# A two-layer conditioned decoder trunk on one core: another order for the opening, swaps of the first rotary tiles by ScalarE, weight loads and score banks arranged anew

## The chip, the cores and the metric

The kernel runs on one core of one Trainium2 chip. The metric is device time in microseconds for one execution of the whole program; lower is better. The engines are named as in the profile: PE (TensorE, matrix products and transposes), DVE (VectorE), ACT (ScalarE), POOL (GpSimd) and SP (SyncE, which here only issues DMAs).

## The reference

Two layers work on `x` (512 rows of 1024, float32), conditioned by a vector `c`:

```python
c_act = silu(c)
for l in range(2):
    ada = c_act @ w_ada[l] + b_ada[l]                  # six pieces of 1024: shift, scale, gate, twice
    h = rmsnorm(x, norm_mix_g[l]) * (1 + sc_m) + sh_m
    a_in, b_in, q, k, v, gate_pre = split(h @ w_in[l])
    y_a, y_b = two convolution branches (a_in, b_in)
    q, k = apply_rope(q, cos, sin), apply_rope(k, cos, sin)   # 8 heads, 2 x 64 each
    o = diff_attention(q, k, v, lam)                   # softmax 0 minus lam * softmax 1, causal
    y_c = rmsnorm(o) @ w_c_out[l]
    x = x + g_m * ((g_a * y_a + g_b * y_b + g_c * y_c) @ w_out[l])
    h = rmsnorm(x, norm_mlp_g[l]) * (1 + sc_f) + sh_f
    x = x + g_f * (relu(h @ w_ff1[l]) ** 2 @ w_ff2[l])
return rmsnorm(x, final_g)
```

The rotary step turns each 64-wide half of a head by an angle `position * inv_freq`: `[t1*cos - t2*sin, t2*cos + t1*sin]`.

## The kernel before

Activations lie transposed: 128 features on the partitions by 512 rows of `x` in the free dimension, so `x` and `h` are 8 tiles of 128x512 each. Every float32 operand is split into a high part (an ACT cast) and a low part (a DVE subtraction), and a product is three passes, high by high, low by high, high by low, of 128x512 matmuls (24 for one output tile of 128 features; `proj`, L145).

**Weights.** `raw_issue` lets SP load 128x8x256 of a weight matrix (1 MB) into one of two `raw` buffers. `w_split` turns one half of a raw buffer (`hh` 0 or 1) into `wh` (ACT, L394) and `wl` (DVE, L402); after the second half it calls `raw_issue`, so the next 1 MB load is issued as soon as the program comes past that point, and waits for the last reader of the buffer.

**Order.** Each engine works through its instructions in the order in which the program emits them. Python generators ("tasks") are spawned with a delay in steps; a step passes with each 4096 columns of matmul (eight 128x512 matmuls). `yield n` in a task lets n steps pass before its next part is emitted. So a task's yields set what stands ahead of what on each queue.

**The opening** is written out by hand, as the string `START` of units. `x` turns a tile of `x` by PE and copies it by ACT (`v`: by DVE), `y` sums squares, `i` loads and turns the parameter rows `prm` (L207), `a` are the steps of the rotary angles (the last one emits the `Sin` activations, sin_t and cos_t), `e` and `d` are the parts of the adaLN products that DVE makes (rows of `w_ada` times a column of `cact`; table `ON_DVE` says how many of 8 k-tiles, for four quarters `qt` and the two vectors scale and shift), `r`, `s` the rest of these products on PE (`rows_of`, L1193), `c`, `t`, `q` copy, turn and store the quarter's result, `m` modulates two tiles of `h`, `h` and `l` split a quarter of the first four weight tiles, and `p` is one of 16 partial products: quarter `qt` of tile `i`. The four tiles are q and k of heads 0 and 1. SP's stream in the opening is 256 KB pieces: positions, 8 of `x`, then per quarter 8 of `w_ada` and 2 of `w_in`. After `START` come 1 MB loads.

**Rotary** (`rope`, L706): ACT copies the product from PSUM, SP issues four DMAs that swap the 32-row groups into `sw`, DVE multiplies by cos_t and, 2 steps later, `sw` by sin_t, adds, and after that the result is split and pieces of it are moved by DMA into the layout of the scores (L738, L739).

**Attention.** `mixer` makes for each pair of heads four product tiles (q, k, q, k), then the values. `attend` makes for each head and row block i of four the scores of both softmaxes (L789, L790), each in a PSUM bank of its own of the two `s` banks:

```python
            sps = [ps_s(), ps_s()]
```

`softmax` masks them on DVE (L754), takes exp on ACT (L761) and combines both on DVE (L770). Then PE turns the combined blocks (L806), and the products with the values follow.

Of the kernel before, what the change touches and what calls it, by code (L numbers as in the profile page):

```python
# [17 lines left out]
P = 128  # L18
# [14 lines left out]
WDELAY = 1  # L33
LAM = 2

ON_DVE = ((2, 3), (1, 5), (8, 3), (3, 7))
START = (
# [4 lines left out]
)  # L42
QSTEP, COMB, AWAIT, PWAIT, PERIOD = 2, 2, 3, 4, 9
CPACE, ADA0, ADA1, APACE = 0.71, 2.36, 2.19, 1.62
ADA_BR = 0
FIRST = 2
RWAIT = 2


RDELAY = (0, 1, 1)  # L50
# [21 lines left out]
def kernel(  # L72
# [158 lines left out]
    def lambdas():  # L231
        lq, lk = slot("at", F32, [1, L, 2, 64]), slot("at", F32, [1, L, 2, 64])
        for j, (a, b) in enumerate(((lam_q1, lam_k1), (lam_q2, lam_k2))):
            G.dma_start(lq[:, :, j, :], a[None, :, :])
            G.dma_start(lk[:, :, j, :], b[None, :, :])
        yield 15
        V.tensor_tensor(lq, lq, lk, op=ALU.mult)
        ls, le, ll = stile(4), stile(4), stile(2)
        V.tensor_reduce(out=ls[0:1, :], in_=lq.rearrange("p l j d -> p (l j) d"), op=ALU.add, axis=AX.X)
        ones = ftile(F32, [1, P])  # L240
        V.memset(ones, 1.0)
        yield 1
        A.activation(le[0:1, :], ls[0:1, :], AF.Exp)
        yield 1
        for l in range(L):
            V.scalar_tensor_tensor(
                out=ll[0:1, l : l + 1], in0=le[0:1, 2 * l + 1 : 2 * l + 2], scalar=-lam_init[l],
                in1=le[0:1, 2 * l : 2 * l + 1], op0=ALU.add, op1=ALU.subtract)
        yield 2
        pt = ps_t()  # L250
        T.matmul(pt[:, 0:2], ones, ll[0:1, :], start=True, stop=True)
        yield 1
        V.tensor_copy(nlam, pt[:, 0:2])
        written.add("lam")
# [103 lines left out]
            chunks += [(len(specs) + g, hh) for hh in range(2) for g in range(len(grp))]  # L358
            specs += grp
    raws, wready = [], []  # L360
    wnext, spare = [0], set()

    def raw_issue():
        if len(raws) < len(specs):
# [6 lines left out]
    def w_split(extra=None):  # L371


        if wnext[0] >= len(chunks):
            return
        n, hh = chunks[wnext[0]]
        wnext[0] += 1
        raw, kk = raws[n], specs[n][2]
        if kk < 0:

            shape, rs = [P, 4, 256], raw[:, 4 * hh : 4 * hh + 4, :]
            n_k = 4
        else:
            shape, rs = [P, 8, P], raw[:, :kk, hh * P : (hh + 1) * P]
            n_k = kk
        if extra:
            half = [P, n_k // 2] + shape[2:]
            his = [slot(extra, F32R, half) for _ in range(2)]
            parts = [(hf, rs[:, i * half[1] : (i + 1) * half[1], :]) for i, hf in enumerate(his)]
        else:  # L390
            hi = wpool.tile(shape, F32R, tag="wh", name=nm("wh"))
            parts = [(hi[:, :n_k, :], rs)]
        for h_, r_ in parts:
            A.copy(h_, r_)  # L394
        yield 1
        if extra:
            los = [slot(extra, F32R, half) for _ in range(2)]
        else:
            lo = wpool.tile(shape, F32R, tag="wl", name=nm("wl"))
            los = [lo[:, :n_k, :]]  # L400
        for l_, (h_, r_) in zip(los, parts):
            V.tensor_tensor(l_, r_, h_.bitcast(F32), op=ALU.subtract)  # L402
        wready.append(([h_[:, k, :] for h_, _ in parts for k in range(n_k // len(parts))],
                       [l_[:, k, :] for l_ in los for k in range(n_k // len(parts))], extra))
        if hh == 1:
            raw_issue()

    def getw():
# [62 lines left out]


    xT = [xpool.tile([P, S], F32, name=f"xT{k}") for k in range(KD)]

    def modulate(l, f, rb, hh, ks, t0=0, t1=S):

        sv = (SH_M if f == 0 else SH_F) * 8
        assert all(q + k in ada_known[l] for k in ks for q in (sv, sv + 8))
        n = t1 - t0
        u = {}  # L480
        for k in list(ks) + [None]:
            if k is not None:
                u[k] = ftile()
                V.scalar_tensor_tensor(
                    out=u[k][:, :n], in0=xT[k][:, t0:t1], scalar=gsc[l][:, f * 8 + k : f * 8 + k + 1],
                    in1=rb[:, :n], op0=ALU.mult, op1=ALU.mult)
                A.activation(hh[k][0][:, t0:t1], u[k][:, :n], AF.Identity,
                             bias=ada[l][:, sv + k : sv + k + 1])
            if len(u) > (1 if k is not None else 0):
                j = min(u)  # L490
                V.scalar_tensor_tensor(
                    out=hh[j][1][:, t0:t1], in0=u.pop(j)[:, :n], scalar=ada[l][:, sv + j : sv + j + 1],
                    in1=hh[j][0][:, t0:t1].bitcast(F32), op0=ALU.add, op1=ALU.subtract)

    def new_h():
        return [(slot("h", F32R), slot("h", F32R)) for _ in range(KD)]
# [207 lines left out]
    cos_t = const.tile([P, S], F32, name="cos_t")  # L704
    sin_t = const.tile([P, S], F32, name="sin_t")

    def rope(pp, res, j):

        t, sw = ftile(), ftile()
        A.copy(t, pp)
        for q in range(4):
            nc.sync.dma_start(sw[32 * q : 32 * q + 32, :], t[32 * (q ^ 1) : 32 * (q ^ 1) + 32, :])  # L714
        yield 1
        u = ftile()
        V.tensor_tensor(u, t, cos_t, op=ALU.mult)
        yield 2
        V.tensor_tensor(sw, sw, sin_t, op=ALU.mult)  # L719
        V.tensor_tensor(u, u, sw, op=ALU.add)  # L720
        yield 1
# [58 lines left out]
    def attend(l, hd, q, k, v, res):  # L780
# [2 lines left out]
        l0 = stile(4)  # L783
        for i in range(NTB):
            n = (i + 1) * P
            sps = [ps_s(), ps_s()]
            blk = slice(i * P, (i + 1) * P)
            for cc in range(2):
                T.matmul(sps[cc][:, :n], q[cc][:, blk], k[cc][:, :n], start=True, stop=False)  # L789
                T.matmul(sps[cc][:, :n], q[2 + cc][:, blk], k[cc][:, :n], start=False, stop=True)  # L790
            spawn(softmax(l, i, sps, l0, a))
            yield QSTEP
# [54 lines left out]
    def mixer(l, h, qk, nfirst):  # L847
# [15 lines left out]
                yield PERIOD  # L863

        spawn(heads())
        for hp in range(NH // 2):
            if hp:
                qk, nfirst = [], 0
# [162 lines left out]
        def branch(pp, br, e, tg):  # L1031
# [6 lines left out]
            else:  # L1038
# [2 lines left out]
                yield 1  # L1041
                yield from split(m[e], merged)

        for br, act in enumerate((oo, yb, ya)):
            hold[0] = False
            if br == ADA_BR and l == 0:
                spawn(ada_task([(0, v) for v in (G_M, SH_F, SC_F, G_F)] +
                               [(1, v) for v in (SC_M, SH_M, G_M, SH_F, SC_F, G_F)], lambda: pace["ada"]))
            for j in range(4):
                tg = []  # L1050
                for e in (2 * j, 2 * j + 1):
                    product(h, gate, br, e, tg)
                    product(act, branch, br, e, tg)
# [45 lines left out]
    rc = const.tile([P, 2], F32, name="rc")  # L1099
    A.dma_start(rc, rope_c)  # L1100
    posi = slot("at", I32)
    nc.sync.dma_start(posi, positions.to_broadcast([P, S]))
    prm_task = params(0)
    next(prm_task)
    x2 = x.rearrange("b s d -> (b s) d")
# [19 lines left out]
    for qt in range(4):  # L1125
        quarters.append((fetch(SC_M, qt), fetch(SH_M, qt)))
        for raw, (src, c0, _) in zip(raws, specs):
            nc.sync.dma_start(raw[:, 2 * qt : 2 * qt + 2, :],
                              src[256 * qt : 256 * qt + 256, c0 : c0 + 256].rearrange("(k p) e -> p k e", p=P))

    pt = ps_t()
    T.transpose(pt[:, :8], crow, ident[:8, :8])
# [38 lines left out]
    def part(qt, v):  # L1171
        return parts[qt % 2][:, v * 256 : v * 256 + 256]

    def partial(qt, vs):

        for k in range(8):
            for v in vs:
                k0 = 8 - ON_DVE[qt][v]
                if k < k0:
                    continue  # L1180
                r = quarters[qt][v][k // 2][:, k % 2, :]
                if k == k0:
                    V.tensor_scalar(out=part(qt, v), in0=r, scalar1=cact[:, k : k + 1],
                                    scalar2=None, op0=ALU.mult)
                else:
                    V.scalar_tensor_tensor(out=part(qt, v), in0=r, scalar=cact[:, k : k + 1],
                                           in1=part(qt, v), op0=ALU.mult, op1=ALU.add)

    def rows_of(qt, v, pt):

# [45 lines left out]
        V.tensor_scalar(out=ms, in0=ms, scalar1=1.0 / D, scalar2=None, op0=ALU.mult)  # L1236
        box["y0"] = rstd(ms, 4)

    w1, qk, q_rows, q_cols, w_tasks = [], [], {}, {}, []
    first = {}  # L1240
    box = {}
    ang_task, lam_task = angles(), lambdas()
# [37 lines left out]
    def first_product(qt, i):  # L1280
# [6 lines left out]
        proj(first[i], w1[i], h, 0, S, 2 * qt, 2 * qt + 2)  # L1287
        if qt == 3:
            release(w1[i])
            spawn(rope(first[i], qk, i))  # L1290
            run_due()

    def rows_scale(qt):
# [3 lines left out]
    def rows_copy(qt):  # L1297
        row = ftile()
        A.copy(row, q_rows[qt])
        q_rows[qt] = row  # L1300

    units = dict(
        x=lambda k: x_turned(k, A),
        v=lambda k: x_turned(k, V),
# [2 lines left out]
        z=lambda _: next(lam_task),  # L1307
        a=lambda _: next(ang_task, None),
        b=lambda _: box.update(rb=bcast(box["y0"], 4)),
        e=lambda qt: partial(qt, (0,)),  # L1310
        d=lambda qt: partial(qt, (1,)),
        f=lambda qt: partial(qt, (0, 1)),
        r=rows_scale,
        s=lambda qt: rows_of(qt, 1, q_rows[qt]),
        c=rows_copy,
        t=lambda qt: q_cols.update({qt: turn(q_rows[qt])}),
        q=lambda qt: quarter_done(qt, q_cols[qt]),
        m=lambda qt: modulate(0, 0, box["rb"], h, (2 * qt, 2 * qt + 1)),
        h=high, l=low,
        p=lambda n: first_product(n // 4, n % 4),  # L1320
    )
# [7 lines left out]
    for l in range(L):  # L1329
# [6 lines left out]
        f = mlp(l, h, f, NF)  # L1336
        if l + 1 < L:
            qk = []
            h = closing(l, G_F, f, l + 1, 0, lambda pp, i: rope(pp, qk, i))
    ending(f)  # L1340
    while tasks:
        step()
# [35 lines left out]
```

## Time and profile before

| | |
|---|---|
| median of 3 runs | 1908.89 us (1908.52 to 1911.45) |
| profiled execution | 1904.28 us, of which 1902.5 us are the span of the trace |
| PE busy | 1874.3 us, 99% of the span |
| DVE, ACT, POOL busy | 1256.0, 785.8, 63.4 us |
| DMA | 241.20 MB, 127 GB/s mean |

The span is the trace from the first to the last instruction; 1.8 us of the profiled execution's time lie around it. A row of the timeline gives the start, the busy time, the engine with the line and operation, output<-input, and in brackets how long the engine sat idle before it and whose event ended that. PE rows of several matmuls overlap in their records, so that a row of six 128x512 matmuls of 0.39 us each lasts 1.53 us.

### The profile page before, as it was taken

The numbers are of one execution on the slowest core, as the hardware profiler recorded it, in microseconds if no ns is written. First come the engines' busy times: TensorE is split into PE (matmuls) and PEld (weight loads), VectorE is DVE, ScalarE is ACT, GpSimd is POOL, SyncE is SP. The second block draws the span as 40 slices with busy tenths as digits, with TensorE's granted clock in tenths as the row PEclk, the third lists the DMA queues.
The fourth block names the chain that finished last, engine by engine and source line by source line (L and its number), as shares of the span: only waits on it lengthen the run. The fifth ranks groups of instructions, "written<-read, shape, count | busy, mean of one in ns | idle before, by whom it ended". The sixth has DMA issues, their size and how long they took to land.

```text
span 1902.5 us, 24972 instructions
## 1 busy us (share of the span) xinstructions
PE 1874.3 (99%) x9565; PEld 1599.9 (84%) x9565; DVE 1256.0 (66%) x2139; ACT 785.8 (41%) x1420; POOL 63.4 (3%) x109
## 2 busy tenths in 40 slices
PE   8999999999999999999999999999999999999998
PEld 6788888888889888888898888888888898888888
DVE  7788789996676556565677777898654563333336
ACT  4466652223333524333445666322243353424253
POOL 1011010000000000000000000000000000000000
PEclk9999999999999999999999999999999999999999
DMA  8644323444554455555535442232233422223221
GB/s 272 181 130 126 101 67 98 151 138 145 166 178 135 139 178 195 177 185 182 171 97 142 123 122 73 89 104 96 67 100 100 133 89 89 89 93 106 89 89 67
DMA packets 211527, 241.20 MB, mean 127 GB/s; under 512 B 10408, under 2 KB 178480, under 8 KB 211408
## 3 DMA queue, kind: packets, MB, share of 16 engines
q1 hardware_dynamic: 210480, 239.38, 40.6%
q8 instruction: 75, 1.23, 0.3%
q0 software_dynamic: 768, 0.23, 0.1%
q14 instruction: 44, 0.36, 0.1%
q10 hardware_dynamic: 160, 0.01, 0.0%
HBM read 216.50 MB, written 2.10 MB: 115 GB/s over the span
## 4 chain that ended last, share of the span: by engine, by line
PE 93%; DMA 3%; DVE 2%; issue 1%; SPq 1%; ACT 1%; POOL 0%; POOLq 0%; DVEq 0%; ACTq 0%
PE mm L145 83%; PE s L145 3%; DMA f<-f 2%; PE t L817 1%; PE s L789 1%; PE s L790 1%; PE t L806 1%; SPq L714 1%; PE t L1193 1%; PE t L455 0%; PE t L303 0%; PE t L825 0%; POOL st L438 0%; DVE f L719 0%; PE t L1214 0%
## 5 line engine op out<-in xcount | busy, mean ns | idle before, releaser
L145 PE MATMUL mm<-h,wh 128*128 128x512 f32 x2720 | 851.3, 392 | 0.0
L145 PEld LDWEIGHTS mm<-h,wh 128*128 128x128 f32 x2720 | 509.6, 188 | 103.3
L145 PE MATMUL mm<-h,wl 128*128 128x512 f32 x1360 | 533.6, 392 | 0.0
L394 ACT CAST wh<-raw 128x1024 fp32r<-128x1024 f32 (+1 forms) x308 | 308.9, 1005 | 407.2 <-PE mm L145 358.2
L402 DVE TENSOR_TENSOR wl<-raw,wh 128x1024 fp32r<-128x1024 f32 (+1 forms) x308 | 358.2, 1166 | 69.6 <-ACT wh L394 65.9
L145 PE MATMUL mm<-qk,wh 128*128 128x512 f32 (+1 forms) x1024 | 300.2, 376 | 0.0
L145 PEld LDWEIGHTS mm<-h,wl 128*128 128x128 f32 x1360 | 256.2, 188 | 51.9
L145 PEld LDWEIGHTS mm<-qk,wh 128*128 128x128 f32 x1024 | 188.2, 188 | 35.1
L145 PE MATMUL mm<-qk,wl 128*128 128x512 f32 (+1 forms) x512 | 192.6, 376 | 0.0
L912 DVE SCALAR_TENSOR_TENSOR cv<-v,caw,cv 128x511 f32<-128x511 f32 (+14 forms) x240 | 176.0, 733 | 4.2
L499 DVE SCALAR_TENSOR_TENSOR xT<-mm,ada,xT 128x512 f32<-128x512 f32 (+1 forms) x81 | 56.0, 691 | 151.2 <-PE mm L145 151.0
L281 DVE SCALAR_TENSOR_TENSOR araw<-araw,cact,araw 128x512 f32<-128x512 f32 x140 | 104.6, 747 | 25.2 <-DMA araw<-in_w_ada_dram 24.7
L145 PEld LDWEIGHTS mm<-qk,wl 128*128 128x128 f32 x512 | 96.3, 188 | 17.2
L1059 ACT ACTIVATE f<-mm 128x512 f32<-128x512 f32 x60 | 35.9, 598 | 160.6 <-PE mm L145 160.6
L145 PE MATMUL mm<-o,wh 128*128 128x512 f32 (+1 forms) x320 | 95.5, 381 | 0.0
L145 PE MATMUL mm<-v,wh 128*128 128x512 f32 (+1 forms) x320 | 94.9, 379 | 0.0
L145 PE MATMUL mm<-wh,h 128*128 128x256 f32 x448 | 84.1, 284 | 0.0
L761 ACT ACTIVATE cv<-cv,st 128x128 f32<-128x128 f32 (+3 forms) x128 | 71.0, 558 | 25.6 <-DVE st L754 25.2
L1033 DVE SCALAR_TENSOR_TENSOR f<-f,mm 128x512 f32<-128x512 f32 x38 | 26.1, 687 | 83.6 <-PE mm L145 83.6
L469 DVE TENSOR_TENSOR qk<-f,qk 128x512 fp32r<-128x512 f32 x38 | 26.3, 691 | 77.4 <-ACT qk L466 77.2
L438 POOL TENSOR_TENSOR st<-st,nhalf 128x4 f32<-128x4 f32 (+2 forms) x29 | 31.2, 1076 | 1368.0 <-DVE st L460 1013.4
L145 PEld LDWEIGHTS mm<-wh,h 128*128 128x128 f32 x448 | 70.8, 191 | 0.4
(259 smaller groups left out, 2282.9 us busy)
## 6 DMA issues: line engine op xcount, KB each, us to landing
raw<-in_w_in_dram SPq DMA_DIRECT2D x66, 1024.0 KB, 5.2
raw<-in_w_ff_dram SPq DMA_DIRECT2D x64, 1024.0 KB, 5.4
araw<-in_w_ada_dram SPq DMA_DIRECT2D x160, 256.0 KB, 3.0
f<-f SPq DMA_DIRECT2D x128, 64.0 KB, 2.0
qk<-qk SPq DMA_DIRECT2D x64, 128.0 KB, 2.6
raw<-in_w_c_out_dram SPq DMA_DIRECT2D x8, 1024.0 KB, 5.0
raw<-in_w_out_dram SPq DMA_DIRECT2D x8, 1024.0 KB, 5.0
qk<-in_w_ada_dram SPq DMA_DIRECT2D x16, 256.0 KB, 6.0
```

What stands on the lines that cost most here:

```text
L145: T.matmul(ps, lhsT, rhs, start=start, stop=stop)
L281: V.scalar_tensor_tensor(out=part, in0=r, scalar=cact[:, k : k + 1], in1=part, op0=ALU.mult, op1=ALU.add)
L394: A.copy(h_, r_)
L402: V.tensor_tensor(l_, r_, h_.bitcast(F32), op=ALU.subtract)
L438: G.tensor_tensor(y, v[:, :n], nhalf[:, :n], op=ALU.pow)
L469: V.tensor_tensor(lo, src, hi.bitcast(F32), op=ALU.subtract)
L499: V.scalar_tensor_tensor(out=xT[e][:, t0:t1], in0=pp[:, t0:t1], scalar=g[:, e : e + 1], in1=xT[e][:, t0:t1], op0=ALU.mult, op1=ALU.add)
L714: nc.sync.dma_start(sw[32 * q : 32 * q + 32, :], t[32 * (q ^ 1) : 32 * (q ^ 1) + 32, :])
L761: A.activation(p[cc][:, :n], p[cc][:, :n], AF.Exp, bias=nb[:, cc : cc + 1], scale=-1.0, accum_out=l0[:, i : i + 1] if cc == 0 else s1)
L912: V.scalar_tensor_tensor(out=ac[:, s:], in0=glu[j][:, : S - s], scalar=wk, in1=ac[:, s:], op0=ALU.mult, op1=ALU.add)
L1033: V.scalar_tensor_tensor(out=t, in0=t, scalar=1.0, in1=pp, op0=ALU.add, op1=ALU.mult)
L1059: A.activation(r, pp, AF.Relu)
```

## The change

The diff has seven parts. First, `START` is another order. The square sums and x turns stand ahead of the parameter rows; 11 small products (`w11`, an identity by itself into an `s` bank) come first on PE; the DVE parts of the adaLN products are emitted for each k-tile by itself (`e02` is quarter 0, k-tile 2), and `ON_DVE` sums to 34 in place of 32; `m` is split into `u` (scale, and the high part by ACT) and `g` (the low part); and `a0` to `a7` stand near the end, behind the last `g`. Second, positions are the last of SP's opening pieces in place of the first. Third, in the opening and in the closing of layer 1, `rope` has `near=True`: ACT makes four copies of 32x512 out of PSUM into the swapped places, no DMA, and DVE multiplies by cos_t straight from PSUM. Fourth, elsewhere the sin product is emitted 3 steps after the cos product in place of 2 (`SWAIT`). Fifth, in the q, k, v stage `w_split` lets 2 steps pass before `raw_issue` (`RAWD`). Sixth, the two scores of a block with up to 256 keys share one `s` bank. Seventh, `lambdas` emits its small product 4 steps after its sums in place of 2.

```diff
-ON_DVE = ((2, 3), (1, 5), (8, 3), (3, 7))
+ON_DVE = ((6, 3), (5, 2), (1, 5), (6, 6))
 START = (
-    "i0 a0 y1 x1 a1 a2 y0 i1 y2 a3 v0 a4 x2 v7 y3 a5 v5 e0 y4 y7 y6 y5 v3 n h2 d0 r0 h0 l2 z "
...
+    "w11 z y2 y1 v1 y0 y7 i0 x4 e02 x3 e03 x7 e04 x0 y5 i1 e05 e06 e07 y3 y6 y4 x5 v2 d05 n d06 r0 "
...
+SWAIT = 3
+RAWD = 2
...
-        yield 2
+        yield 4
         pt = ps_t()
         T.matmul(pt[:, 0:2], ones, ll[0:1, :], start=True, stop=True)
...
         if hh == 1:
+            if rdelay[0]:
+                yield rdelay[0]
             raw_issue()
...
-        t, sw = ftile(), ftile()
-        A.copy(t, pp)
-        for q in range(4):
-            nc.sync.dma_start(sw[32 * q : 32 * q + 32, :], t[32 * (q ^ 1) : 32 * (q ^ 1) + 32, :])
+        sw = ftile()
+        if near:
+            t = pp
+            for q in range(4):
+                A.copy(sw[32 * q : 32 * q + 32, :], pp[32 * (q ^ 1) : 32 * (q ^ 1) + 32, :])
+        else:
+            t = ftile()
+            A.copy(t, pp)
+            for q in range(4):
+                nc.sync.dma_start(sw[32 * q : 32 * q + 32, :], t[32 * (q ^ 1) : 32 * (q ^ 1) + 32, :])
         yield 1
         u = ftile()
         V.tensor_tensor(u, t, cos_t, op=ALU.mult)
-        yield 2
+        yield 1 if near else SWAIT
...
-            sps = [ps_s(), ps_s()]
+            sps = [ps_s()]
+            sps.append(ps_s() if n > 256 else sps[0][:, n:])
...
         spawn(heads())
+        rdelay[0] = RAWD
...
+        rdelay[0] = 0
         for br, act in enumerate((oo, yb, ya)):
...
-    nc.sync.dma_start(posi, positions.to_broadcast([P, S]))
...
+    nc.sync.dma_start(posi, positions.to_broadcast([P, S]))
...
-            spawn(rope(first[i], qk, i))
+            spawn(rope(first[i], qk, i, True))
...
+    def scaled(k):
+        u_[k] = ftile()
+        V.scalar_tensor_tensor(out=u_[k], in0=xT[k], scalar=gsc[0][:, k : k + 1], in1=box["rb"],
+                               op0=ALU.mult, op1=ALU.mult)
+        A.activation(h[k][0], u_[k], AF.Identity, bias=ada[0][:, SH_M * 8 + k : SH_M * 8 + k + 1])
+
+    def scaled_low(k):
+        V.scalar_tensor_tensor(out=h[k][1], in0=u_.pop(k), scalar=ada[0][:, SH_M * 8 + k : SH_M * 8 + k + 1],
+                               in1=h[k][0].bitcast(F32), op0=ALU.add, op1=ALU.subtract)
...
-            h = closing(l, G_F, f, l + 1, 0, lambda pp, i: rope(pp, qk, i))
+            h = closing(l, G_F, f, l + 1, 0, lambda pp, i: rope(pp, qk, i, True))
```

What this moves is seen in three places. In the rows below, a name's last number tells one buffer from the next; `t` are PSUM banks for turns, `f` work tiles.

PE at the program's start, before, where f_123 holds the parameter rows, cv_126 to cv_132 pieces of x:

```order
L1132 MATMUL t_216<-ident,f_116 128x8
L207 MATMUL t_253<-ident,f_123 128x56
L1214 MATMUL t_259<-ident,cv_126 128x128
L1214 MATMUL t_259<-ident,cv_128 128x128
L1214 MATMUL t_259<-ident,cv_130 128x128
```

and after:

```order
L1128 MATMUL t_216<-ident,f_116 128x8
L1225 MATMUL s_253<-ident 128x128 x11
L1208 MATMUL t_275<-ident,cv_125 128x128
L1208 MATMUL t_275<-ident,cv_127 128x128
L1208 MATMUL t_275<-ident,cv_129 128x128
L1208 MATMUL t_275<-ident,cv_131 128x128
L211 MATMUL t_285<-ident,f_122 128x56
```

The turn of the parameter rows no longer stands ahead of the first turn of x, and 11 products stand where PE had none.

ACT at the end of the opening, before, from the last high part of `h` on (raw_584 is the first whole 1 MB load, mm_444, s_456 and s_422 hold finished first products, wh_638 is a weight half that the value products need):

```order
L487 ACTIVATE h_238<-f_607,ada_99 128x512
L712 COPY f_624<-mm_444 128x512
L394 CAST cv_632<-raw_584 128x512
L394 CAST cv_633<-raw_584 128x512
L394 CAST wh_638<-raw_584 128x1024
L712 COPY f_646<-s_456 128x512
L394 CAST wh_674<-raw_599 128x1024
L712 COPY f_680<-s_422 128x512
```

and after (raw_547 is the first whole load now, wh_644 stands for wh_638):

```order
L398 CAST cv_595<-raw_547 128x512
L398 CAST cv_596<-raw_547 128x512
L1161 ACT_TABLE_LOAD
L1161 ACTIVATE sin_t<-at_222,rc 128x512
L1162 ACTIVATE cos_t<-at_223 128x512
L702 COPY f_637<-mm_474 32x512 x4
L398 CAST wh_644<-raw_547 128x1024
```

The table load, sin and cos, which stood some 20 rows earlier, stand now behind the casts of the load's first half and ahead of the copies and of the cast wh_644.

SP in the second pair of heads of layer 1, before (f_917 and f_990 are swapped tiles of the pair's first two products):

```order
L714 DMA f_917<-f_916 32x512 x4
L367 DMA raw_963<-in_w_in_dram 128x8x256
L367 DMA raw_970<-in_w_in_dram 128x8x256
L714 DMA f_990<-f_989 32x512 x4
L738 DMA qk_1015<-qk_1015 64x512
```

and after (f_919 and f_994 are these tiles now):

```order
L707 DMA f_919<-f_920 32x512 x4
L707 DMA f_994<-f_995 32x512 x4
L371 DMA raw_1012<-in_w_in_dram 128x8x256
L371 DMA raw_1014<-in_w_in_dram 128x8x256
L731 DMA qk_1039<-qk_1039 64x512
```

The two weight loads stand behind the second group of swaps. On ACT the cast of the first of them stands, before, behind two casts of q and the exps of block 2:

```order
L712 COPY f_989<-mm_923 128x512
L723 CAST qk_1015<-f_941 128x512
L724 CAST qk_1016<-f_941 64x512
L761 ACTIVATE cv_985,st_877<-cv_985,st_984 128x384
L761 ACTIVATE cv_987,st_1019<-cv_987,st_984 128x384
L394 CAST wh_1022<-raw_963 128x1024
L761 ACTIVATE cv_1045,st_877<-cv_1045,st_1044 128x512
```

and after it stands right behind the copy whose swaps the load is queued behind:

```order
L705 COPY f_995<-mm_926 128x512
L398 CAST wh_1021<-raw_1012 128x1024
L716 CAST qk_1039<-f_952 128x512
L717 CAST qk_1040<-f_952 64x512
L754 ACTIVATE cv_1017,st_866<-cv_1017,st_1016 128x512
L754 ACTIVATE cv_1019,st_1043<-cv_1019,st_1016 128x512
L705 COPY f_1072<-mm_1001 128x512
```

The exps of block 3 follow that cast in both, but in the second program the casts of q do as well.

More of the change, by code (lines that the diff above doesn't have):

```diff
@@ L360 @@
     raws, wready = [], []
-    wnext, spare = [0], set()
+    wnext, spare, rdelay = [0], set(), [0]
     def raw_issue():
@@ L473 @@
     xT = [xpool.tile([P, S], F32, name=f"xT{k}") for k in range(KD)]
[L475 to L493, printed above, removed]
     def new_h():
@@ L705, with rope @@
     sin_t = const.tile([P, S], F32, name="sin_t")
-    def rope(pp, res, j):
-        t, sw = ftile(), ftile()
-        A.copy(t, pp)
-        for q in range(4):
-            nc.sync.dma_start(sw[32 * q : 32 * q + 32, :], t[32 * (q ^ 1) : 32 * (q ^ 1) + 32, :])
+    def rope(pp, res, j, near=False):
+        sw = ftile()
[8 more added lines that the diff above has]
+                nc.sync.dma_start(sw[32 * q : 32 * q + 32, :], t[32 * (q ^ 1) : 32 * (q ^ 1) + 32, :])
         yield 1
@@ L1172, in part, with partial @@
         return parts[qt % 2][:, v * 256 : v * 256 + 256]
[L1174 to L1187, printed above, removed]
+    def partial(qt, k, v):
+        k0 = 8 - ON_DVE[qt][v]
+        if k < k0:
+            return
+        r = quarters[qt][v][k // 2][:, k % 2, :]
+        if k == k0:
+            V.tensor_scalar(out=part(qt, v), in0=r, scalar1=cact[:, k : k + 1],
+                            scalar2=None, op0=ALU.mult)
+        else:
+            V.scalar_tensor_tensor(out=part(qt, v), in0=r, scalar=cact[:, k : k + 1],
+                                   in1=part(qt, v), op0=ALU.mult, op1=ALU.add)
     def rows_of(qt, v, pt):
@@ L1237, in rms @@
         box["y0"] = rstd(ms, 4)
-    w1, qk, q_rows, q_cols, w_tasks = [], [], {}, {}, []
+    w1, qk, q_rows, q_cols, w_tasks, u_ = [], [], {}, {}, [], {}
     first = {}
@@ L1309 @@
         b=lambda _: box.update(rb=bcast(box["y0"], 4)),
-        e=lambda qt: partial(qt, (0,)),
-        d=lambda qt: partial(qt, (1,)),
-        f=lambda qt: partial(qt, (0, 1)),
+        e=lambda n: partial(n // 10, n % 10, 0),
+        d=lambda n: partial(n // 10, n % 10, 1),
         r=rows_scale,
@@ L1317 @@
         q=lambda qt: quarter_done(qt, q_cols[qt]),
-        m=lambda qt: modulate(0, 0, box["rb"], h, (2 * qt, 2 * qt + 1)),
+        u=scaled, g=scaled_low,
         h=high, l=low,
```

8 rows, old and new, of the table START are left out of this document.

## The prediction

> **What bounds the kernel now.** I read the busy line and the chain of the page first, then the waits of PE, then the timeline of the two stages that the change touches.
>
> ```profile
> PE 1874.3 (99%) x9565; PEld 1599.9 (84%) x9565; DVE 1256.0 (66%) x2139; ACT 785.8 (41%) x1420; POOL 63.4 (3%) x109
> PE 93%; DMA 3%; DVE 2%; issue 1%; SPq 1%; ACT 1%; POOL 0%; POOLq 0%; DVEq 0%; ACTq 0%
> PE t L207 <- DMA f<-in_norm_mix_g_dram: 6.1, 1, 6.1
> PE s L789 <- DVE st L754: 5.6, 5, 2.2
> PE s L789 <- DMA qk<-f: 3.4, 2, 3.2
> PE t L251 <- DVE st L246: 0.8, 1, 0.8
> ```
>
> PE is the bound, and 93% of the chain is PE's own work. That work hardly changes. So the change can win little more than the waits listed (total us, times, longest), and it loses wherever another engine gets so late that PE waits anew. I look for both.
>
> **Opening, up to the last first product.**
>
> ```profile
> 8.64 0.32 PE L207 MATMUL t<-ident,f 56*128 56x56 f32 x1 [6.13 <-DMA f<-in_norm_mix_g_dram]
> 8.89 5.47 PE L1214 MATMUL t<-ident,cv 128*128 128x128 f32 x24
> 33.73 1.01 DVE L1186 SCALAR_TENSOR_TENSOR part<-o,cact,part 128x256 f32<-128x256 f32 x2 [0.48 <-DMA o<-in_w_ada_dram]
> 28.32 3.61 DVE L1186 SCALAR_TENSOR_TENSOR part<-o,cact,part 128x256 f32<-128x256 f32 x7
> 50.41 1.42 DVE L491 SCALAR_TENSOR_TENSOR h<-f,ada,h 128x512 fp32r<-128x512 f32 x2
> 51.74 0.42 DVE L1276 TENSOR_TENSOR wl<-raw,wh 128x256 fp32r<-128x256 f32 x1
> 15.00:28.60 13.60, 13.46 (x69) 11.38 (x68) 11.71 (x32) 7.34 (x16) 3.34 (x5) 1.00 1.10 347
> 28.60:52.00 23.40, 23.40 (x111) 19.43 (x110) 21.68 (x52) 9.87 (x20) 3.51 (x7) 1.00 0.67 211
> 0.00:21.00 21.00, 0.00 (x0) 0.00 (x0) 5.68 (x11) 0.00 (x0) 2.29 (x4) 1.00 0.92 296
> 58.10 1.60 PE L145 MATMUL mm<-cv,h 128*128 128x256 f32 x12
> ```
>
> (The rows with two times are stretches: length, then busy time and instructions of PE, weight load, DVE, ACT, POOL, clock, DMA share, GB/s. The last of them counts the `at` tiles alone, which are the angles: 5.68 us of DVE.) PE now idles 6.13 us behind the parameter rows, and its first turns take 5.47/24 = 0.23 us each. The change lets PE start at the first of x, with warm-up products before it. This is worth up to 6 us at that place. I cost it at nothing for the end of the opening: before, the last products end at 58.10, 6.3 us behind DVE's last low half (50.41 + 1.42 = 51.83), and after, DVE's list sets that again. In its new order quarter 2 starts with the fourth scale piece. A 256 KB piece takes 0.755 us at 347 GB/s. The eighth piece of that quarter ended a wait of DVE at 33.73, so the fourth lands four pieces earlier, and one more since positions go last: 29.9, or 28.6 should the stream pause behind it rather than before. From there DVE has 4 first parts (0.35 each, an estimate from the 0.42 of the same size), 14 further ones (3.61/7 = 0.52), 10 weight lows (0.42, less back to back: 3.9 in all), 13 modulate operations (0.71) and 9 small ones (under 0.2 each): 23 us. The last low half is done at 51.6 to 52.9, as before, although the angles are gone from ahead of it: DVE lacked data earlier, not time. Two fewer PE products (30 for 32 of adaLN) save under 1 us. First products end at 58: 0, with -2.5 to +1 as bounds (-2.5 if the stream runs on).
>
> **Angles behind the norm.** The 5.68 us now stand on DVE behind 52, and what waits for them is on ACT.
>
> ```profile
> 27.11 1.28 ACT L1165 ACT_TABLE_LOAD   x1
> 28.40 0.72 ACT L1165 ACTIVATE sin_t<-at,rc 128x512 f32<-128x512 f32 x1
> 29.03 0.61 ACT L1166 ACTIVATE cos_t<-at 128x512 f32<-128x512 f32 x1
> 53.87 0.59 ACT L712 COPY f<-mm 128x512 f32<-128x512 f32 x1 [2.83 <-PE mm L145]
> 54.35 1.14 ACT L394 CAST cv<-raw 128x512 fp32r<-128x512 f32 x2
> 55.39 1.05 ACT L394 CAST wh<-raw 128x1024 fp32r<-128x1024 f32 x1
> 57.22 1.15 DVE L402 TENSOR_TENSOR wl<-raw,wh 128x1024 fp32r<-128x1024 f32 x1
> 59.65 0.28 PE L145 MATMUL mm<-wl,h 128*128 128x256 f32 x1
> 70.91 0.63 PE L145 MATMUL mm<-h,wh 128*128 128x512 f32 x2
> 76.10 0.30 PE L789 MATMUL s<-qk,qk 128*128 128x128 f32 x1 [3.19 <-DMA qk<-f]
> raw<-in_w_in_dram SPq DMA_DIRECT2D x66, 1024.0 KB, 5.2
> qk<-f SPq DMA_DIRECT2D x32, 128.0 KB, 2.3
> ```
>
> Sin and cos were ready at 29.6. Now: the first whole load waits for the last use of its buffer, a weight low 1.8 us ahead of DVE's end, so is issued at 50.2, lands 5.2 later at 55.4, and its casts (two in 1.14) end at 56.5. DVE does half of the angles (3.1 us, to 55.1), stands behind those casts for two lows of the load (1.3, to 57.3 to 57.8), and does the rest (2.6): 60 to 60.4. Sin and cos are done at 61. Behind them on ACT stand the four copies of the first rotary tile and only then the cast wh_644. A copy of 32x512 has no row; the nearest is 128x512 with 0.59, or 0.48 from start to start (53.87, 54.35), so four take 1.9 to 2.4; below that only if fewer partitions are faster. wh_644 is cast at 64.2, its low half at 65.3. PE wants it at 59.65: it stalls some 5.6 us, 4 if everything of this meets its lower end, where before it did not wait. The values' remaining products took from 59.65 to 70.91 less 0.76 for the product of `lambdas` (that wait goes): PE is through at 76, and at 77 with the clock's recovery, which is priced in the next part.
>
> The scores of head 0 then need q and k. From 61 ACT has ahead of the last cast: four tiles of copies (8.4), three wh (3.15), a table load and exp (1.5), three casts of q and k (0.62 each): 14.9, to 75.9; a DVE subtraction of 0.69 and 2.3 of DMA follow: 78.9. Before, scores began at 76.10 with eight matmuls done ahead of them that now come later (1.8): 74.3 on the same count. So **+4.5**, with +2 to +6. It contains the 3.19 us wait, which the ScalarE swaps were to shorten and which returns with another cause.
>
> [...] The row of the cosine product's old input is the copy at 53.87; after the change that product reads the bank itself. [...]
>
> **Loads two steps later.** The second pair of heads, before:
>
> ```profile
> 85.82 1.51 SPq L367 DMA_DIRECT2D raw<-in_w_in_dram  x2
> 89.07 0.59 ACT L712 COPY f<-mm 128x512 f32<-128x512 f32 x1 [3.27 <-PE mm L145]
> 89.68 2.43 SPq L714 DMA_DIRECT2D f<-f  x4
> 92.05 1.03 ACT L394 CAST wh<-raw 128x1024 fp32r<-128x1024 f32 x1
> 93.12 1.23 DVE L402 TENSOR_TENSOR wl<-raw,wh 128x1024 fp32r<-128x1024 f32 x1 [1.03 <-ACT wh L394]
> 94.26 0.69 DVE L754 CUSTOM_DVE_ANT_0 cv<-s,mask 128x512 f32<-128x512 f32 x1
> 95.71 0.71 ACT L761 ACTIVATE cv<-cv,st 128x512 f32<-128x512 f32 x1
> 99.98 0.75 DVE L770 SCALAR_TENSOR_TENSOR cv<-cv,st,cv 128x512 f32<-128x512 f32 x1
> 101.23 0.60 PE L806 MATMUL t<-ident,cv 128*128 128x128 f32 x4
> 102.90 0.39 PE L789 MATMUL s<-qk,qk 128*128 128x256 f32 x1 [1.07 <-DVE st L754]
> 73.40:77.40 4.00, 1.17 (x5) 1.09 (x6) 3.41 (x8) 1.47 (x4) 0.41 (x1) 0.88 0.79 211
> 1028.86 1.05 PE L145 MATMUL mm<-h,wh 128*128 128x512 f32 x2
> ```
>
> The loads were issued ahead of the second swaps; now SP issues them after these, at 92.1. The first lands at 97.3 (5.2), and ACT, whose queue has its cast right behind the copy, waits from 89.7 to 97.3. The cast ends at 98.4, not 93.1: 5.3 us later. Queued behind it on ACT are two casts of q and both exps of block 3, on DVE the low half and then the masks of block 3, which start at 99.6 in place of 94.26. The exps end near 101.8, and the combination, which ended at 100.7, ends between 103 (right behind the exps) and 105.4 (with the same 3.6 us of rotary work between). PE's turns of that block stood at 101.2 to 101.8: a stall of 1.5 to 4.5; I take 4, since that rotary work is still there. After a long wait the clock drops: the stretch with the 3.19 us wait has 0.88 in it, and the matmuls that follow it cost about 1.4 us more. Against this stand the 1.07 and a wait of 0.9 further on, which go: **+3.4**, with -1 to +4.
>
> On that clock: behind the 2.2 us wait among those on masks, the last row, two 128x512 matmuls take 1.05, where they take 0.63 at 70.91, so the trace has the clock fall after 2.2 us. [...]
>
> The two later pairs of layer 1 and three of layer 2 have the same queue. Where exps stand ahead of the cast only DVE is held. Each pair costs from 0 (slack covers it; PE does not wait for casts there now) to the 3.4 of the second pair. I take 1 each in layer 1 and 2 in layer 2, where pairs hold scores on masks now: **+8**, with 0 to +17.
>
> **One score bank for two.** Of the 5.6 us that PE waits on masks, 4.5 lie outside the second pair, and the 2.2 us one among them costs clock too. Blocks 0 and 1 then have a bank each and no wait: **-5.2**; 0 if the masks themselves come late.
>
> **The rest.** The sine product a step later (eight matmuls, 1.8 us) delays q and k of a pair; the heads' own period covers it, and if not, scores wait up to 1.8 a pair. The copies in the closing of layer 1 add 3 x 1.5 us of ACT, which is idle there for over half of the time. In the branch stage loads are undelayed. All at 0.
>
> **Sum.** 0 + 4.5 + 3.4 + 8 - 5.2 = +10.7, less 0.7 for the two adaLN products: +10. On the profiled execution's 1904.3 that is 1914.3; it lay 4.6 under the median of the runs, so on the median 1908.9 + 10 = **1919**.
>
> **The rivals.** *The late loads are covered* (faster): all six pairs have the slack, so the casts' 5.3 us never reach PE. Then 3.4 and 8 become -2 and 0, and the sum is 4.5 - 2 - 5.2 - 0.7 = -3.4, with the angles' end 1.5 to 2.5 earlier -5 to -6: 1903 to 1905.5. For it: PE waits for no cast in any pair now. Against it: combination and turn lie 0.5 us apart in the second pair, less than the delay; from a slack of 5.3 it decides. *It evens out*: the second pair stalls, the later ones do not, +3.4 + 4.5 - 5.2 - 0.7 = +2, 1911, or less. *Worse*: every pair stalls as the second and sharing banks gives nothing: 4.5 + 3.4 + 17 - 0.7 = +24; half of the later pairs, +16, 1925. *The angles do not hold PE*, the rest as forecast: 1914.5.
>
> **How the numbers follow.** Forecast with the case of no angle wait, 1913 to 1924: 0.45. Covered: 0.25, of which a part ends within 0.2%. Evens out: 0.15. Worse: 0.15. 0.2% (3.8 us) is about what a measurement tells from no change. Faster 0.25, same 0.17, slower 0.58. The range leaves out half of the worst and the best end of the covered: 1902 to 1926; the forecast's own is 1913 to 1924.
>
> **What would show it.** In the trace after: sin_t starting near 60; PE waiting about 5 us for a low half inside the first values product; scores of head 0 near 79; ACT idle 7 us behind the second copy of each pair with a load as releaser; PE waiting at L800 in the second pair. If sin_t starts before 57, or PE passes that turn without a wait, I am wrong. Right for the shared bank is that no score waits on a mask.

## The result, and the profile after

The changed kernel is slower: 1926.79 us (median of 4 runs, 1926.32 to 1929.6) against 1908.7 (4 runs of before, 1904.95 to 1911.45). The two medians alone give a ratio of 1.0095; the ratio given with the result is 1.0108 with an interval of 1.0096 to 1.012. Forecast was 1919, range 1902 to 1926, so the time lies just outside of it. The direction and the path through the late loads were right, the size was not: +18 measured for +10 (+20.6 by that ratio).

The busy line and the chain of the page after, then the waits of PE (total us, times, longest):

```profile
PE 1883.5 (98%) x9583; PEld 1606.5 (83%) x9583; DVE 1255.7 (65%) x2140; ACT 796.2 (41%) x1442; POOL 62.2 (3%) x109
PE 90%; DMA 3%; DVE 3%; ACT 2%; issue 1%; SPq 0%; POOL 0%; POOLq 0%; DVEq 0%; ACTq 0%
PE mm L149 <- ACT wh L398: 4.9, 1, 4.9
PE s L783 <- DVE st L747: 4.8, 2, 2.8
PE t L819 <- ACT o L815: 4.4, 2, 2.7
PE t L800 <- DVE cv L763: 4.2, 2, 2.3
PE t L800 <- DVE subg L216: 4.0, 1, 4.0
PE s L783 <- issue: 2.2, 1, 2.2
PE mm L149 <- DVE wl L406: 1.1, 1, 1.1
```

The 6.1 us behind the parameter rows and the waits of layer 1's scores on masks are gone. In their place PE waits for a weight half in the first values product (4.9 and 1.1), for the turns of softmax blocks (L800, 8.2 in all), for masks in layer 2, and for turns of the heads' outputs (L819).

To see where the time goes, I added up PE's lost time by stage: from row to row of PE's timeline, the distance between ends less the usual one of that shape (0.227 us for 128x512, 0.12 for 128x256, 0.109 for 128x128). Waits and half-clock matmuls (granted clock 0.50, as from 109.5 to 113 after) are both in it.

| PE's lost time, us | before | after | after, no load delay |
|---|---|---|---|
| layer 1, pair 1: values | 1.1 | 8.6 | 8.4 |
| pair 2: q, k (with head 0's scores) | 5.5 | 9.8 | 3.6 |
| pair 2: values | 2.4 | 0.1 | 0.9 |
| pairs 3 and 4 | 0.8 | 7.0 | 0.8 |
| layer 2, pairs 2 to 4 | 6.8 | 12.7 | 1.1 |

The last column belongs to the first experiment below. The opening is left out of the table, because its matmuls have other usual distances; it ends at 58.3, 58.3 and 58.6 us, so what PE won at its start did not reach its end. Outside these stages the three agree within 0.4 us.

The chain that the prediction followed stands in the timeline of ACT and DVE after, at the end of the opening:

```profile
51.07 0.75 DVE L1303 SCALAR_TENSOR_TENSOR h<-f,ada,h 128x512 fp32r<-128x512 f32 x1
55.69 1.14 ACT L398 CAST cv<-raw 128x512 fp32r<-128x512 f32 x2 [5.45 <-DMA raw<-in_w_in_dram]
59.92 0.72 ACT L1161 ACTIVATE sin_t<-at,rc 128x512 f32<-128x512 f32 x1 [1.79 <-DVE at L1159]
61.17 2.34 ACT L702 COPY f<-mm 32x512 f32<-32x512 f32 x4
63.54 1.04 ACT L398 CAST wh<-raw 128x1024 fp32r<-128x1024 f32 x1
63.55 0.69 DVE L710 TENSOR_TENSOR f<-mm,cos_t 128x512 f32<-128x512 f32 x1 [3.32 <-ACT f L702]
64.64 0.58 PE L149 MATMUL mm<-wh,h 128*128 128x256 f32 x1 [4.91 <-ACT wh L398]
80.84 0.30 PE L783 MATMUL s<-qk,qk 128*128 128x128 f32 x1 [2.25 <-issue]
```

The last low half ends at 51.8, as before; the cast waits for the late first load, sin for DVE's late angles, and the weight half stands behind sin, cos and four copies. A copy of 32x512 took 2.34/4 = 0.59 us, what one of 128x512 took before (0.59 at 53.87): a quarter of the partitions saved nothing. And the second pair of heads of layer 1:

```profile
94.48 0.56 ACT L705 COPY f<-mm 128x512 f32<-128x512 f32 x1
95.07 2.65 SPq L707 DMA_DIRECT2D f<-f  x4
95.81 0.68 DVE L747 CUSTOM_DVE_ANT_0 cv<-s,mask 128x512 f32<-128x512 f32 x1
97.83 1.17 SPq L371 DMA_DIRECT2D raw<-in_w_in_dram  x2
103.16 1.05 ACT L398 CAST wh<-raw 128x1024 fp32r<-128x1024 f32 x1 [8.12 <-DMA raw<-in_w_in_dram]
105.40 0.72 ACT L754 ACTIVATE cv<-cv,st 128x512 f32<-128x512 f32 x1
108.72 0.75 DVE L763 SCALAR_TENSOR_TENSOR cv<-cv,st,cv 128x512 f32<-128x512 f32 x1
109.52 0.48 PE L800 MATMUL t<-ident,cv 128*128 128x128 f32 x1 [4.02 <-DVE subg L216]
```

ACT stands 8.12 us with its cast at the head of its queue, the exp of block 3 behind it, then the combination on DVE, then PE's turn, whose wait ends with that combination (the name given is another DVE event that came last by the semaphores). ACT has such a wait in the q, k stage of pairs 2 to 4 of both layers, six in all, 8.0 to 9.0 us each; without the load delay it is 1.1 to 1.6.

### The profile page after: what moved, and what is told of

Read it like the earlier page. It is cut to its first block, busy times and chain, and to the rows that moved or that the text cites. A ratio compares the mean times of both kernels' runs of the same rounds, so it can differ in the third digit from the quotient of the medians.

```text
span 1924.6 us, 24944 instructions
## 1 busy us (share of the span) xinstructions
PE 1883.5 (98%) x9583; PEld 1606.5 (83%) x9583; DVE 1255.7 (65%) x2140; ACT 796.2 (41%) x1442; POOL 62.2 (3%) x109
## 4 chain that ended last, share of the span: by engine, by line
PE 90%; DMA 3%; DVE 3%; ACT 2%; issue 1%; SPq 0%; POOL 0%; POOLq 0%; DVEq 0%; ACTq 0%
PE mm L149 81%; PE s L149 3%; DMA raw<-in_w_in_dram 2%; PE t L811 1%; PE s L783 1%; PE t L800 1%; PE s L784 1%; ACT wh L398 1%; DMA qk<-in_w_ada_dram 1%; DVE wl L406 0%; PE t L307 0%; PE t L461 0%; DVE cv L747 0%; PE t L819 0%; ACT cv L754 0%
```

## The experiments

The medians of before differ by 0.2% between the result and the three groups of experiments (1908.7, 1905.9, 1905.1, 1905.7), so each experiment's ratio is to before on the same chip.

**1. After without the load delay.**

```diff
-RAWD = 2
+RAWD = 0
```

> The changed kernel (1926.8 us) with RAWD = 0, so that the 1 MB loads of the q, k, v stage are issued without the two steps of delay; all else stays. Load theory (the delayed loads hold ACT and DVE, and with them PE's turns of the softmax blocks, in every pair of heads): PE's waits from the second pair on, some 12 us more than before the change, go, and the time is 1915, 1913 to 1917; what is left over 1908.7 is the angles'. Rival (the later sine product or the shared bank makes those waits): the turns wait as long as now and the time stays at 1924 to 1928.

1904.23 us; 0.999 of before, 0.9977 to 1.0002. The time lies far below the 1913 to 1917 that I expected: the load delay costs 1926.8 - 1904.2 = 22.6 us (22.5 by the two ratios), twice what I had for it. The same stretch of the timeline:

```profile
91.42 1.93 SPq L371 DMA_DIRECT2D raw<-in_w_in_dram  x2
96.57 1.06 ACT L398 CAST wh<-raw 128x1024 fp32r<-128x1024 f32 x1 [1.33 <-DMA raw<-in_w_in_dram]
```

ACT waits 1.33 us for the load in place of 8.12. Over the whole program ACT's waits on loads at this line, first after, then without the delay, are

```profile
ACT wh L398 <- DMA raw<-in_w_in_dram: 77.1, 15, 9.0
ACT wh L398 <- DMA raw<-in_w_in_dram: 32.9, 15, 4.1
```

44 us less of ACT's waiting is worth 22.6 of PE's time: half had been covered.

**2. Before with the load delay alone** (`rdelay` with 2 steps in the q, k, v stage).

> The kernel before (1908.7 us) with the two steps of delay of the loads in the q, k, v stage as the only change. Load theory: PE waits at the turn of the last softmax block in the second pair of layer 1 for 3 to 4 us and in the later pairs for 1 to 3 each; 1919, 1916 to 1922. Rival (the delay harms only together with the later sine product or the shared bank): 1907 to 1911.

1938.64 us; 1.017 (1.0152 to 1.0187), against the 1919 that I expected. It costs +32 us on the old kernel. PE's waits there, and ACT's copy and cast in the second pair of layer 1:

```profile
PE s L791 <- DVE st L756: 15.9, 11, 3.6
PE t L808 <- DVE cv L772: 9.0, 3, 4.3
PE s L791 <- DMA qk<-f: 7.0, 2, 4.4
90.84 0.59 ACT L714 COPY f<-mm 128x512 f32<-128x512 f32 x1 [3.25 <-PE mm L145]
99.61 1.04 ACT L394 CAST wh<-raw 128x1024 fp32r<-128x1024 f32 x1 [5.69 <-DMA raw<-in_w_in_dram]
```

Scores wait on masks in eleven places. The delay needs no company to harm. On ACT two casts of q and both exps of block 2 stand between that copy and the cast, and still ACT waits 5.69 us for the load. Why the delay costs 10 us less in the changed kernel, no run here separates.

**3. After with the angles early.** Positions first on SP, `a0` to `a6` among the early DVE parts, `a7` behind `c1`.

> The changed kernel (1926.8 us) with the positions first on SP again and the steps of the angles spread over the early opening, sin and cos behind the copy of quarter 1's row; all else as after. Theory of the late angles: the waits of 4.9 and 1.1 us for a weight half in the first values product go, and the scores of head 0 begin some 5 us earlier against the values' end; 1921, 1918 to 1923. Rival (DVE has no room before the norm, so that the last first products end as much later as the angles take, 5 us): 1925 to 1930.

1926.92 us; 1.0109 (1.0093 to 1.0124): nothing won. By stage, the values product lost 2.6 us in place of 8.6, but the opening ended at 59.9 for 58.3, and the stage of pair 2 lost 13.2 for 9.8. What the angles had cost was there, 6 us, and came back in two places. The opening took 1.6 us. The other 3.4 went into the first scores of head 0, which start at 78.14 in place of 80.84 but behind a longer wait, 3.93 us for 2.25, with slow matmuls after it (1.05 us for two, where the two at 82.55 after took 0.62):

```profile
78.14 0.30 PE L778 MATMUL s<-qk,qk 128*128 128x128 f32 x1 [3.93 <-issue]
79.08 1.05 PE L144 MATMUL mm<-h,wh 128*128 128x512 f32 x2
```

The wait of the turn on the late load hardly moved (4.21 us for 4.02). The time lies in the rival's range, but not for the rival's reason: the opening ends 1.6 us later, not 5. The theory had the place right and the sum wrong.

**4. Before with the shared score bank alone.**

```diff
-            sps = [ps_s(), ps_s()]
+            sps = [ps_s()]
+            sps.append(ps_s() if n > 256 else sps[0][:, n:])
```

> The kernel before (1908.7 us) with the two scores of a block of up to 256 keys in one bank as the only change. Prediction's term: the waits of scores on masks (5.6 us in five places, 1.4 of clock) go: 1903, 1901 to 1905. Rival (the wait only moves on, to block 2, which then needs both banks at once, or to the turns): 1907 to 1911.

1904.33 us; 0.9988 (0.9978 to 0.9999), some 2 us. The time fits the prediction's term, the trace the rival. The waits on masks went where I had put them, in layer 2's second pair 4.1 us of lost time became 0.2; but in the values stage behind it 0.0 became 4.1, and in layer 1's second values stage 2.4 became 4.3. The wait moved on.

**5. After with one step of delay** (`RAWD = 1`): on SP the loads of the second pair stand ahead of the second swaps, on ACT nothing moves.

> The changed kernel (1926.8 us) with RAWD = 1 in place of 2. On SP the two loads of the second pair of heads then stand ahead of the second group of swaps again, as with RAWD = 0 (1904.2 us), and ACT's rows are in the same order in all three. Theory of the place on the queue (what costs is that a load stands behind a swap group, and the swap group behind ACT's copy, with ACT's cast of that load right behind the copy): all of it goes, 1904 to 1907. Rival (each step of delay costs in proportion): half of the 22.6 us stays, 1913 to 1918.

1904.68 us; 0.9992 (0.9982 to 1.0002). The whole cost is gone:

```profile
92.81 1.92 SPq L371 DMA_DIRECT2D raw<-in_w_in_dram  x2
96.66 2.41 SPq L707 DMA_DIRECT2D f<-f  x4
98.13 1.06 ACT L398 CAST wh<-raw 128x1024 fp32r<-128x1024 f32 x1 [1.49 <-DMA raw<-in_w_in_dram]
```

It is not the steps, it is the swap group that the load stands behind.

**6. After, two steps of delay, loads issued by POOL** in the q, k, v stage.

```diff
-            nc.sync.dma_start(raw[:, : abs(kk), :],
+            (nc.gpsimd if rdelay[0] else nc.sync).dma_start(raw[:, : abs(kk), :],
```

> The changed kernel (1926.8 us), RAWD = 2 as it is, but in the q, k, v stage POOL issues the 1 MB loads in place of SP. They then wait for the buffer's last reader, not for the swaps ahead of them on SP's queue. Theory of the place on the queue: most of the 22.6 us that separate 1926.8 from 1904.2 go, 1904 to 1910, the more of it the sooner the buffers come free. Rival (the load is late because its buffer is, or POOL's own work ahead holds it as long): 1920 to 1928.

1904.01 us; 0.9993 (0.9984 to 1.0002). With the delay as it was, on a queue without swaps, nothing is lost:

```profile
92.74 0.95 POOL L371 DMA_DIRECT2D raw<-in_w_in_dram  x1 [10.68 <-DMA f<-f]
98.74 1.05 ACT L398 CAST wh<-raw 128x1024 fp32r<-128x1024 f32 x1 [2.08 <-DMA raw<-in_w_in_dram]
```

The load leaves at 92.7 (91.4 without delay, 97.8 with the delay on SP), and ACT waits 2.08 us. POOL's row names a swap as what ended its wait, but DVE's last read of the buffer ended at 92.45, and the second load too left 0.3 us behind its own buffer's last read. With the fifth experiment this settles the cause: a load queued on SP behind a swap group that itself waits for ACT's copy, while ACT's queue comes to the cast of that load before the load can land. The cast need not stand right behind the copy: in the second experiment two casts and two exps stand between, and the delay costs more.

**7. Before with the shared bank and the later sine product in the pairs.**

```diff
-            product(h, rope, qk, j)
+            product(h, rope, qk, j, 3)     # steps between cosine and sine product; rope's default stays 2
```

> The kernel before (1905.9 us on the chip of the shared bank's run, where the shared bank alone gave 1904.3) with the shared bank and, in the pairs of heads alone, the sine product 3 steps after the cosine product. Theory A (the later sine product frees DVE from waiting for swaps, so that masks come in time; this is what lets the shared bank win): PE's waits on masks and on turns of blocks, 7 to 9 us by the stages of the changed kernel without load delay, go: 1897 to 1901. Rival (the later product adds nothing): 1903 to 1906.

1897.98 us; 0.996 (0.9947 to 0.9972). Faster than before by 7 us, as theory A had it, though the next but one shows that its share for the bank was wrong.

**8. After, no load delay, angles early.**

> The changed kernel without load delay (RAWD = 0: 1904.2 us) and with the angles early, positions first. Theory (the late angles cost what the first values product waits for a weight half, 6 us less of it with angles early, hidden in the run with load delay by what came behind): 1898 to 1901. Rival (the opening's end comes later by as much, or q and k of head 0 are late all the same): 1903 to 1906.

1902.23 us; 0.9983 (0.9974 to 0.9991). Against 1904.2, 2 us of the expected 3 to 6: between the two theories. The opening ends at 61.4 (58.6 with late angles), the values lose 2.5 us (8.4), and pair 2 loses 6.7 (3.6). DVE lacks the room for part of the angles, and scores of head 0 wait longer, 3.90 us for 2.38:

```profile
79.50 0.30 PE L778 MATMUL s<-qk,qk 128*128 128x128 f32 x1 [3.90 <-issue]
```

**9. Before with the later sine product alone.**

> The kernel before (1905.1 us on the chip of the last runs) with the later sine product in the pairs of heads alone, and a bank for each score. With the shared bank as well it took 1898.0, the shared bank alone 1904.3. If only both together win (the bank takes away the wait on masks, the sine product the waits that come in its place): 1903 to 1906, PE waiting on masks as before. Rival (the later sine product alone frees DVE, and the bank adds nothing): 1897 to 1900.

1896.26 us (1895.07 to 1897.69, 5 runs); 0.9948 (0.9934 to 0.9961). The rival holds: one `yield` wins 9 us, and the bank adds nothing to it that can be told (0.9948 and 0.996 lie within each other's intervals). It is the fastest version found, and beats both kernels. DVE's waits on swapped tiles at the sine product, before and here:

```profile
DVE f L719 <- DMA f<-f: 13.5, 10, 2.6
DVE f L719 <- DMA f<-f: 6.5, 7, 2.1
```

and PE has no wait on masks left in its list:

```profile
PE t L207 <- DMA f<-in_norm_mix_g_dram: 6.6, 1, 6.6
PE s L789 <- DMA qk<-f: 3.5, 2, 3.3
PE t L455 <- POOL st L438: 2.8, 3, 0.9
```

Seven us less of DVE waiting at the head of its queue went together with the end of all 5.6 us that PE waited for masks, and of the half clock behind the longest of them (0.50 from 1028.8 to 1030 before). In five of the ten waits before, 8.5 us of the 13.5, a mask is among the next few instructions of DVE; those of pairs 2 to 4 of layer 2 are among them. The first of these:

```profile
1026.34 0.69 DVE L719 TENSOR_TENSOR f<-f,sin_t 128x512 f32<-128x512 f32 x1 [1.95 <-DMA f<-f]
1027.07 0.69 DVE L720 TENSOR_TENSOR f<-f,f 128x512 f32<-128x512 f32 x1
1027.67 0.28 DVE L754 CUSTOM_DVE_ANT_0 cv<-s,mask 128x128 f32<-128x128 f32 x1
```

**10. After, no load delay, two banks.**

> The changed kernel without load delay (1904.2 us) with a bank for each score again. If the shared bank is what offsets the late angles there: PE waits on masks, above all in layer 2 (2 us and clock in its first pair, 0.5 to 1 in two others), and the time is 1909 to 1912. Rival (the later sine product did it): 1903 to 1906.

1906.04 us; 0.9999 (0.999 to 1.0008), not to be told from 1904.2 with 0.999. In the profile 1.7 us of lost time come back in layer 2's second pair. The rival holds here as well; a share of the bank of up to some 2 us is not excluded.

**11. The kernel of experiment 7 (kernel 7 from here on) with the first swaps by ScalarE.**

> The kernel of the shared bank and later sine product on the old opening (1898.0 us) with the first four tiles' swaps as four ScalarE copies each. In it scores of head 0 wait 4.5 us for q and k. Change's idea: without the swaps' DMAs (2.0 us each from issue to landing) q and k come 2 us sooner or more: 1895 to 1897. Prediction's view (ACT's four copies, 2 us a tile for 0.6, and DVE's cosine product behind them cost as much): 1898 to 1901.

1897.49 us; 0.9951 (0.9939 to 0.9964): the same as kernel 7. Pair 2's stage loses 4.5 us in place of 7.2, the values stage 2.4 in place of 0.7. Inconclusive between the two theories, since the interval is wider than what parts them.

**12. Kernel 7 with head 0 two steps later.**

> The kernel of the shared bank and later sine product on the old opening (1898.0 us) with head 0 started two steps later in each layer (FIRST = 4 for 2), so that 16 more matmuls stand ahead of its scores. If the 4.5 us wait for q and k and its clock are a matter of order alone, 3.6 us of it are filled: 1893 to 1895. Rival (the heads behind it and the turns of their blocks are late by as much): 1897 to 1900.

1897.2 us; 0.9954 (0.9942 to 0.9967): no gain. The 4.5 us wait for q and k is gone, pair 2's stage loses 0.9 in place of 7.2, but the branch stage behind layer 1's pairs loses 5.7 in place of 0.7, since the last head is late:

```profile
252.36 0.50 PE L790 MATMUL s<-qk,qk 128*128 128x512 f32 x1 [2.37 <-DVE st L754]
253.45 1.05 PE L145 MATMUL mm<-h,wh 128*128 128x512 f32 x2
```

## Why the prediction missed the size

**Opening: right.** First products end at 58.3 in both (forecast 58), although PE began without the 6.1 us wait. The forecast's reason, that DVE lacked data and not time, is half right: with the angles back in the early opening the end moves by 1.6 us (experiment 3) and 2.8 (experiment 8), so that part of their 5.7 us found DVE idle and part did not.

**Angles: right in place, near in size.** Forecast sin_t at 60, the end of the weight half's cast at 64.2, a stall of 5.6, scores at 78.9; measured 59.92, 64.58 (63.54 + 1.04), 4.9 + 1.1, 80.84. The sum over the parts other than loads (+4.5 - 2 - 5.2 - 0.7 = -3.4) came out at 0.999 of before in the first experiment, -2 us. That it came so near was luck: what the first experiment's kernel has beyond kernel 7 (the new opening, closing and `lambdas`; 0.999 against 0.996) costs about 6 us, of which early angles give back 2, and the sine product, forecast at nothing, pays for it.

**Loads two steps later: the step that failed, by its size.** In the second pair the sizes held: forecast were 7.6 us of ACT's wait and a PE stall of 4; measured 8.1 and 4.0. By the table that pair loses 5.4 us more with the delay than without, as much as 4 and 1.4 of clock (granted 0.50 from 109.5 to 113). One link of that path was wrong without harm: the masks of block 3 do not stand behind the late low half, they start at 95.81, ahead of it, and the delay reaches that turn through the exps. The later pairs were forecast at +8 by taking 1 of 3.4 in layer 1 and 2 of 3.4 in layer 2, "from 0 (slack covers it)". There was no row for that slack. By the table the two later pairs of layer 1 lose 6.2 us (forecast 2), and the three of layer 2 lose 11.6 (forecast 6): there one late cast holds first the masks and then, through them, two score blocks. After, in layer 2's second pair:

```profile
1043.44 1.05 ACT L398 CAST wh<-raw 128x1024 fp32r<-128x1024 f32 x1 [8.79 <-DMA raw<-in_w_in_dram]
1044.52 1.23 DVE L406 TENSOR_TENSOR wl<-raw,wh 128x1024 fp32r<-128x1024 f32 x1 [7.25 <-ACT wh L398]
1046.22 0.44 PE L783 MATMUL s<-qk,qk 128*128 128x384 f32 x1 [1.93 <-DVE st L747]
1049.68 0.69 PE L783 MATMUL s<-qk,qk 128*128 128x384 f32 x1 [2.84 <-DVE st L747]
```

In all the delay costs 22.6 us for a forecast of 13.4 (5.4 + 8; the 3.4 of the sum is the 5.4 less 2 us of old waits). So the later pairs, 17.8 us by the table for a forecast of 8, are 9.8 short, and that alone is more than the miss of 8 (+18 for +10). What failed is the assumption of slack: ACT's wait is as long in the later pairs as in the second, and PE pays for it in each. The rival of covered loads was excluded by this; the load terms of the worst case, 3.4 + 17 with every pair as the second, come nearest.

**Shared bank and later sine product: nearly the right sum, the wrong owner.** I gave -5.2 to the bank and 0 to the sine product. Alone, the bank is worth -1.6 us (experiment 4) and the sine product -9.4 (experiment 9). The sign that I gave for the bank, no score waiting on a mask, holds without the load delay (experiment 1), but the bank alone leaves two such waits, 2.7 us (experiment 4). I had asked only who waits longer for q and k, and not what DVE stops waiting for: the profile had ten waits of it for swapped tiles, 13.5 us, and masks close behind five of them.

**The copies: right.** The cosine product, which reads the bank itself, starts at 63.55, 0.04 us behind the end of the last copy (61.17 + 2.34 = 63.51), with ACT as its releaser. The copies cost the upper end, 2.34.

## What to carry to other kernels

To price a transfer that is issued late, look at what stands at the head of the queue of the engine that waits for it, and at everything in that queue which another engine needs. Here the consumer's cast soon came up on ACT, the load on SP stood behind swaps that waited for ACT, and one step less of delay, or another issuing queue, brought the whole 22.6 us back. The same reading gives gains: emitting a DVE product one step later behind its DMA, so that it more often finds the data there, won 9 us on a kernel in which DVE was busy for 66% of the time.

Slack that no row shows should not be halved into a sum: either quote its row, pair by pair, or take the whole delay as one end and say so.

## What was not expected of the hardware

In these runs the clock does not fall at a fixed length of wait. Before, two matmuls behind a wait of 2.16 us took 1.05 us, and so they did in experiment 12 behind one of 2.37 us (shown there); after, behind one of 2.31 us in layer 1's third pair, they ran at full speed. The wait of before, whose slow matmuls the prediction shows, then the two rows of after:

```profile
1028.02 0.39 PE L789 MATMUL s<-qk,qk 128*128 128x256 f32 x1 [2.16 <-DVE st L754]
159.86 0.33 PE L800 MATMUL t<-ident,cv 128*128 128x128 f32 x1 [2.31 <-DVE cv L763]
161.40 0.63 PE L149 MATMUL mm<-h,wh 128*128 128x512 f32 x2
```

The granted clock is 0.61 from 1028.0 to 1031.4 before, 0.63 from 252.36 to 256 in experiment 12, and 1.00 from 159.8 to 163 after. The prediction's reading, a clock that falls after 2.2 us of waiting and costs about 1.4 us, was too simple; what decides between such waits stays open.
